# Attention of a two-layer decoder step: the low halves of the split keys are stored by GpSimd instead of SyncE

## The chip, the core and the metric

The kernel runs on one core of a Trainium2 chip. The metric is the device time of one execution in microseconds (us); for the kernel before it is 1973.53 us, the median of three runs from 1971.57 to 1974.1 us. An execution with the hardware profiler gives the views that are quoted below; its own time was 1971.77 us, its span from first to last instruction 1970.0 us.

## The reference

One inference step of a two-layer trunk on 1024 new prompt tokens and 8 sample tokens (one new token each for eight old sequences), width 1024. Layer 0 is a gated linear recurrence, layer 1 grouped-query attention over a window of 128 tokens, 16 query heads on 4 key heads of 64 channels, with a learned sink per head; a squared-ReLU MLP with 4096 hidden channels follows each. The part that the change touches is the norm of queries and keys and the product of the two:

```python
def qkv_heads(x, w_qkv, q_g, k_g):
    q, k, v = jnp.split(x @ w_qkv, [Q_DIM, Q_DIM + KV_DIM], axis=-1)
    q = rms_norm(q.reshape(n, t, N_KV, GROUP, HEAD_DIM), q_g)
    k = rms_norm(k.reshape(n, t, N_KV, HEAD_DIM), k_g)
    v = v.reshape(n, t, N_KV, HEAD_DIM)
...
    s = jnp.einsum('...qkgd,...skd->...kgqs', q, k).astype(jnp.float32) * (HEAD_DIM ** -0.5)
    s = s - alibi_slopes()[:, :, None, None] * dist.astype(jnp.float32)
    s = jnp.where(mask, s, NEG_INF)
```

Everything is float32.

## The kernel before

**Layout.** Activations lie with channels on the 128 partitions and the 1032 tokens (1024 and 8) along the free axis, eight tiles for the width. The tokens are worked on in three thirds of 344 columns (`cs(c)` is the slice of third c). Float32 products are made of float32r pieces: each operand is split into a high part (a cast, on ScalarE, called ACT in the profile) and a low part (the value less the high part, on VectorE, called DVE), and a product is three matmuls, high by high, high by low and low by high (`passes`, line 229).

**Weights.** They come from HBM in units of 128x1024, 512 KB, in one fixed order: for the attention k 0, q 0, k 1, v 0, v 1, q 1, q 2 and so on to q 7. `fetch` (line 166, the DMA is at L173) loads a unit into a tile `raw` from a ring of two buffers, issued by SyncE (SP); `split_unit` (line 175) makes the parts, in two halves each: a cast on ACT (L179) and a subtraction on DVE (L180). `ensure` and `unit` (lines 210 and 221) keep this some units ahead of the products. So the third unit in a row can be loaded only when the first has been split.

**Start of the attention.** `proj_many` (line 259, called at line 1140) projects, for each third in turn, the first pair of key heads (k 0) and then the first query tile (q 0): 24 matmuls each, recorded at L240. Then `proj_steps` (line 922, matmuls at L928) projects the second pair of key heads (k 1), third by third; `by_token` (line 357) computes factors for the values; `v_proj` (line 948, matmuls at L958) the values; and from line 1147 on the query tiles 1 to 7 are projected in between the blocks of the attention (`stage_a`, line 994, matmuls of queries by keys at L1003).

**What follows a projected third of keys.** `take_out` (line 843) takes it out of its bank by two instructions on ACT, a square (L845) and a copy (L846). `k_norm` (line 849) sums the squares of a head with a plain float32 matmul (L852), then DVE L853, ACT L306, L307, L308 and DVE L309, L311 make the factor. `k_evac` (line 901) multiplies (DVE L911), and `parts` (line 861) splits into `hi` (ACT L863) and the low part, which is left in `x` itself (DVE L864). Each part is then stored four times by DMAs from SBUF to SBUF (L915): the two heads of the pair (`own`, 64 partitions each) are each put into the lower and the upper half of a tile of their own, `kh` for the high and `kl` for the low parts. These are the tiles that L1003 reads. There are 2 pairs, 3 thirds and 8 stores of 86.0 KB for each: 48 stores. A projected third of queries goes through `q_evac` (line 870): a square (L875), a cast `hi` (L877), the low part `lo` (DVE L878), and four stores into the query tiles (L884, L885).

**What sets the order.** Each engine takes its instructions in program order, and the scheduler of the framework writes that order: it puts all instructions that are ready into a simulated order by priority, so an edit on one queue can move instructions on others. A DMA stands in the order of the engine that issues it, and waits there for its source, its target and its semaphore (8 of them in rotation for the DMAs of SP and ACT, 8 for those of GpSimd, called POOL). The small tiles of 128x344 (`S`: squares, `x`, `hi`, `lo`, factors) share 9 buffers; a buffer is free again when the stores that read it have landed.

Of the kernel before, what the change touches and what calls it, by code (L numbers as in the profile page):

```python
# [65 lines left out]
def trunk(ctx: ExitStack, tc: tile.TileContext, I, O):  # L66
    nc = tc.nc
    pe, act, dve, pool, sp = nc.tensor, nc.scalar, nc.vector, nc.gpsimd, nc.sync
# [36 lines left out]
    def A(s="a"):  # L105
        return A2(s)[:, 0:T]
# [4 lines left out]
    def S(s="s"):  # L111
        return small["pool"].tile([P, CH], F32, tag="S", name=nm(s))
# [27 lines left out]
    def cs(c):  # L140
        return slice(c * CH, (c + 1) * CH)
# [683 lines left out]
    def attention(hs):  # L825
# [23 lines left out]
        def k_norm(sx, e):  # L849
            s, x = sx  # L850
            st = B("N")[:, :CH]
            pe.matmul(st, lhsT=blk, rhs=s, start=True, stop=True)  # L852
            dve.scalar_tensor_tensor(s, e, fx["e4"], st, ALU.mult, ALU.add)  # L853
            return x, rstd_m2(s, eps=fx["e2"])

        kst = {}
# [4 lines left out]
        def parts(x):  # L861
            hi = S("hi")
            last["k act"] = act.copy(r_(hi), x).ins  # L863
            last["k dve"] = dve.tensor_tensor(r_(x), x, hi, ALU.subtract).ins  # L864
            return hi, x
# [35 lines left out]
        def k_evac(p, c, o, e):  # L901
            if c == 0:
                kst[p] = [(A("kh"), A("kl")) for _ in range(2)]
            x, r = k_norm(o, e)
            if c == 2:
                o = 2 * CH
                kout = S("kout")[:, :P + NS]
                dve.scalar_tensor_tensor(kout, x[:, SEQ - P - o:T - o], fx["kg"], r[:, SEQ - P - o:T - o], ALU.mult, ALU.mult)
                sp.dma_start(O["k"][p], kout[:, :P])
                pool.tensor_copy(ks[:, p, :], kout[:, P:P + NS])  # L910
            dve.scalar_tensor_tensor(x, x, qg[:, 0:1], r, ALU.mult, ALU.mult)  # L911
            for n, x in enumerate(parts(x)):
                for u, own in enumerate((lower, upper)):
                    for half in (lower, upper):
                        sp.dma_start(kst[p][u][n][half, cs(c)], x[own, :])  # L915
            if c == 2:
                done.add(("k", p))

# [219 lines left out]
        with tc.issue_after(last["c0"]):  # L1138
            wk, wq = unit("k", 0, 1), unit("q", 0, 1)
        proj_many([wk, wq], hs, lambda i, c, o: q_evac(0, c, o) if i else k_evac(0, c, take_out(o), fx["row"][:, cs(c)]))  # L1140
        run(proj_steps(unit("k", 1, 1), lambda c, o: k_evac(1, c, take_out(o), fx["row"][:, cs(c)]), iter(())))
        by_token()
        v_proj()
# [44 lines left out]
        for j in range(NJ):  # L1188
# [6 lines left out]
            n = max(0, int((j + 1 - j1) * r) - int((j - j1) * r)) if j < J0 or j >= J1 else 0  # L1195
# [375 lines left out]
```

## Time and profile before

| what | value |
|---|---|
| median of the runs | 1973.53 us (1971.57 to 1974.1, 3 runs) |
| profiled execution | 1971.77 us, span 1970.0 us |
| TensorE (PE) busy | 1958.6 us, 99% of the span |
| DVE, ACT, POOL busy | 1493.6, 1009.1, 363.9 us |
| the 48 stores of L915 | issued by SP from 988.2 to 1032.5 us, about 0.59 us each, landing 2.1 us after the issue (median) |
| PE from 985 to 1045 us | busy 57.66 of 60 us |

A row of a timeline gives the start in us from the begin of the span, the duration in us, the engine, the line of the kernel, the operation with its output and inputs (buffer numbers left out) and the count of merged instructions; in brackets stands how long the engine was idle just before, and what it waited for. "SPq" is SP issuing. A busy PE can still be a PE in which matmuls overlap: the start of one to the start of the next is what a matmul costs. A row of waits gives who waited, for whom, the total, the times and the longest. The landing of a DMA is counted from its issue.

### The profile page before, as it was taken

What the parts mean: (1) busy time and instruction counts of PE and PEld (TensorE: products, weight loads), DVE (VectorE), ACT (ScalarE), POOL (GpSimd) and SP (SyncE); (2) the same over time, 40 slices, a digit from 0 to 9 for tenths busy, and PEclk for the clock granted to TensorE, in tenths of its full rate; (3) what the DMA queues carried; (4) which work ended last, traced back from release to release, by engine and by line L of the source; (5) the groups of instructions that cost most, each with busy time, mean ns of one, the idle gap of its engine ahead of it and who ended that gap; (6) DMA issues with size and microseconds to landing.
All of it is one profiled execution on the core that took longest, in us unless ns stands there. A gap on an engine that the chain in (4) does not pass through costs nothing.

```text
span 1970.0 us, 34847 instructions
## 1 busy us (share of the span) xinstructions
PE 1958.6 (99%) x13004; PEld 1828.2 (93%) x13004; DVE 1493.6 (76%) x3006; ACT 1009.1 (51%) x1985; POOL 363.9 (18%) x618
## 2 busy tenths in 40 slices
PE   9999999999999999999999999999999999999999
PEld 9999999999999899999999998999999999999998
DVE  8896747987777888777744778579877779688784
ACT  6476636443434655554544667455443436455552
POOL 2330000000001233321003667100000003223321
PEclk9999999999999999999999999999999999999999
DMA  5111242244445798988353335612444447788886
GB/s 183 43 44 54 78 156 83 108 153 154 144 153 196 215 243 209 238 199 202 123 143 90 109 89 192 216 65 86 173 140 156 140 176 261 200 205 220 225 207 180
DMA packets 116537, 308.07 MB, mean 156 GB/s; under 512 B 17544, under 2 KB 47248, under 8 KB 116368
## 3 DMA queue, kind: packets, MB, share of 16 engines
q0 software_dynamic: 29568, 102.07, 21.6%
q1 hardware_dynamic: 56272, 131.34, 20.4%
q10 hardware_dynamic: 30528, 72.45, 10.3%
q8 instruction: 102, 1.67, 0.3%
q14 instruction: 67, 0.55, 0.1%
HBM read 177.95 MB, written 115.16 MB: 149 GB/s over the span
## 4 chain that ended last, share of the span: by engine, by line
PE 94%; DVE 2%; DMA 2%; ACT 1%; issue 1%; SPq 0%; POOL 0%; DVEq 0%; ACTq 0%
PE bD L605 36%; PE bZ L605 26%; PE bP L240 11%; PE bS L240 7%; PE bP L928 4%; PE bT L240 3%; PE bS L1003 2%; PE bO L1053 1%; PE bS L958 1%; PE bT L1030 1%; PE bP L1030 1%; DMA x<-xT 0%; PE bN L890 0%; DVE sq L291 0%; DVE hl L1256 0%
## 5 line engine op out<-in xcount | busy, mean ns | idle before, releaser
L605 PEld LDWEIGHTS bD<-op,op 128*128 128x128 f32 x3072 | 380.6, 188 | 8.1 <-DVE ho L753 0.3
L605 PE MATMUL bD<-op,op 128*128 128x260 f32 x3072 | 383.2, 283 | 0.0
L605 PEld LDWEIGHTS bD<-tl,op 128*128 128x128 f32 x2880 | 362.3, 188 | 11.8 <-DVE ho L753 0.6
L605 PE MATMUL bD<-tl,op 128*128 128x260 f32 x2880 | 366.5, 283 | 0.1
L618 POOL DMA_DIRECT2D tl<-hsum x210 | 123.6, 661 | 892.0 <-PE bD L605 409.8
L452 ACT CAST op<-ws 128x512 fp32r<-128x512 f32 (+2 forms) x288 | 158.7, 561 | 248.7 <-DVE ws L573 125.2
L605 PE MATMUL bZ<-op,op 128*128 128x512 f32 x1152 | 282.3, 395 | 0.8 <-DVE y L414 0.8
L605 PE MATMUL bZ<-tl,op 128*128 128x512 f32 x1080 | 272.2, 395 | 0.2 <-DVE tl L460 0.2
L605 PEld LDWEIGHTS bZ<-op,op 128*128 128x128 f32 x1152 | 210.6, 188 | 44.5 <-DVE y L414 1.1
L605 PEld LDWEIGHTS bZ<-tl,op 128*128 128x128 f32 x1080 | 194.6, 188 | 37.8 <-DVE tl L460 0.7
L460 DVE TENSOR_TENSOR tl<-tl 128x520 fp32r<-128x520 f32 (+1 forms) x210 | 136.5, 692 | 76.7 <-ACT tl L459 76.5
L452 ACT CAST op<-raw 128x512 fp32r<-128x512 f32 (+2 forms) x216 | 120.9, 561 | 133.8 <-PE bD L605 71.5
L453 DVE TENSOR_TENSOR op<-ws,op 128x512 fp32r<-128x512 f32 (+2 forms) x288 | 171.4, 610 | 7.6 <-ACT op L452 7.5
L453 DVE TENSOR_TENSOR op<-raw,op 128x512 fp32r<-128x512 f32 (+2 forms) x216 | 131.6, 611 | 9.6 <-ACT op L452 8.7
L753 DVE TENSOR_TENSOR ho<-bD,ho 128x520 f32<-128x520 f32 x140 | 97.5, 696 | 37.0 <-PE bD L605 36.1
L459 ACT CAST tl<-tl 128x520 fp32r<-128x520 f32 (+1 forms) x210 | 117.6, 626 | 2.2 <-DMA tl<-hsum 0.8
L180 DVE TENSOR_TENSOR wl<-raw,wh 128x512 fp32r<-128x512 f32 (+1 forms) x73 | 64.3, 895 | 35.9 <-ACT wh L179 19.2
L743 DVE TENSOR_TENSOR ho<-bZ,ho 128x512 f32<-128x512 f32 x72 | 49.6, 688 | 43.8 <-PE bZ L605 43.5
L727 ACT COPY he<-bZ 128x512 f32<-128x512 f32 x72 | 42.0, 583 | 75.4 <-PE bZ L605 69.4
L745 ACT COPY he<-bZ 128x512 f32<-128x512 f32 x68 | 39.9, 586 | 77.5 <-PE bZ L605 65.3
L753 DVE TENSOR_TENSOR he<-bD,he 128x520 f32<-128x520 f32 x71 | 49.4, 696 | 38.9 <-PE bD L605 38.7
L1016 ACT ACTIVATE se<-se,den 128x257 f32<-128x257 f32 (+1 forms) x128 | 62.9, 494 | 30.0 <-DVE den L1013 22.6
(365 smaller groups left out, 3950.7 us busy)
## 6 DMA issues: line engine op xcount, KB each, us to landing
raw<-w_up SPq DMA_DIRECT2D x64, 512.0 KB, 3.8
tl<-hsum POOLq DMA_DIRECT2D x120, 260.0 KB, 6.7
raw<-w_dn SPq DMA_DIRECT2D x64, 384.0 KB, 6.9
tl<-hsum POOLq DMA_DIRECT2D x90, 256.0 KB, 6.7
spill<-ho POOLq DMA_DIRECT2D x32, 516.0 KB, 6.7
spill<-he POOLq DMA_DIRECT2D x32, 516.0 KB, 6.5
hsum<-ts ACTq DMA_DIRECT2D x30, 520.0 KB, 4.0
hsum<-ho ACTq DMA_DIRECT2D x30, 516.0 KB, 3.6
```

What stands on the lines that cost most here:

```text
L180: eng.tensor_tensor(r_(lo[:, sl]), raw[:, sl], hi[:, sl], ALU.subtract)
L240: pe.matmul(o, lhsT=r_(wt[:, col(k):col(k) + P]), rhs=r_(xt[:, cs(c)]), start=(k == first and a == 0), stop=(k == final and a == 2))
L452: act.copy(r_(hi), x)
L453: dve.tensor_tensor(r_(lo), x, hi, ALU.subtract)
L459: act.copy(r_(hi), lo)
L460: eng.tensor_tensor(r_(lo), lo, hi, ALU.subtract)
L605: pe.matmul(d[:, 512 * b:512 * b + c], lhsT=r_(wt[:, j * P:j * P + P]), rhs=r_(xt[:, c * b:c * b + c]), start=first and j == 0 and a == 0, ...
L618: pool.dma_start(t[:, n:2 * n], src)
L743: dve.tensor_tensor(o0, d, o[:, HP], ALU.add)
L753: last["sum"] = dve.tensor_tensor(t, inner(d), t, ALU.add).ins
L928: pe.matmul(o, lhsT=r_(wt[:, k * P:k * P + P]), rhs=r_(xt[:, cs(c)]), start=(k == 0 and a == 0), stop=(k == M8 - 1 and a == 2))
L1016: act.activation(se[:, u, 256 - n:257], se[:, u, 256 - n:257], AF.Exp, scale=-1.0, bias=dn[:, u:u + 1], accum_out=dn[:, 2 + u:3 + u])
```

## The change

The four stores of a low part (`n` is 1 in the loop over `parts`) are issued by GpSimd, those of the high part by SP as before. 24 of the 48 stores move; what they copy is the same.

```diff
@@ -912,7 +912,7 @@
             for n, x in enumerate(parts(x)):
                 for u, own in enumerate((lower, upper)):
                     for half in (lower, upper):
-                        sp.dma_start(kst[p][u][n][half, cs(c)], x[own, :])
+                        (pool if n else sp).dma_start(kst[p][u][n][half, cs(c)], x[own, :])
             if c == 2:
                 done.add(("k", p))
```

The scheduler's order moves with it. On SP, at the first third of k 0 and q 0: `kh_10468` to `kl_10471` are the key tiles, `q_10519` and `q_10520` the query tiles, and `raw_10885` is the unit q 1 of the weights, which PE needs only for the second query tile.

```order
 L915 DMA kh_10470<-hi_10483 64x344 x2
-L915 DMA kl_10469<-x_10465 64x344 x2
-L915 DMA kl_10471<-x_10465 64x344 x2
+L173 DMA raw_10885<-w_qkv 128x1024
 L884 DMA q_10519<-hi_10523 64x344
 L885 DMA q_10519<-lo_10524 64x344
 L884 DMA q_10520<-hi_10523 64x344
 L885 DMA q_10520<-lo_10524 64x344
-L173 DMA raw_10885<-w_qkv 128x1024
```

The load of the unit q 1 now stands right behind the four stores of the high part; it stood behind four more of the low part and four of the query.

On ACT, in the second third: `wh_10895` is the high part of that unit q 1, `sq_10521`, `hi_10571` and `hi_10608` belong to the second third of q 0 and k 0, `sq_10641` and `x_10642` are the square and the copy of the last third of k 0.

```order
 L308 ACTIVATE q_10564<-r_10563 128x344
+L179 CAST wh_10895<-raw_10885 128x512 x2
 L875 ACTIVATE sq_10521<-bT_10582 128x344
 L863 CAST hi_10571<-x_10557 128x344
 L877 CAST hi_10608<-bT_10582 128x344
-L179 CAST wh_10895<-raw_10885 128x512 x2
 L845 ACTIVATE sq_10641<-bP_10616 128x344
 L846 COPY x_10642<-bP_10616 128x344
```

The two casts of the unit q 1, which stood right ahead of the square of the last third, stand three instructions earlier.

On PE, in the last third of q 0 (`bP_10671`), the matmul L852 of that square stands two matmuls earlier; the order of DVE is the same throughout. On POOL the stores fill a stretch that held only the copies of the last keys (L910):

```order
 L355 DMA st<-msrow 8x1
+L915 DMA kl_10469<-x_10465 64x344 x2
+L915 DMA kl_10471<-x_10465 64x344 x2
+L915 DMA kl_10469<-x_10557 64x344 x2
+L915 DMA kl_10471<-x_10557 64x344 x2
 L910 COPY st<-kout_10655 128x8
+L915 DMA kl_10469<-x_10642 64x344 x2
+L915 DMA kl_10471<-x_10642 64x344 x2
```

Further on in ACT's order, where the second third of k 1 is taken out, the row of the changed kernel with its waits reads as follows; DMASW are the semaphores of POOL's DMAs, and before the change this copy had no wait of its own.

```order
L845 ACTIVATE sq_10795<-bP_10770 128x344 [waits DMAHW3_49,DMAHW2_49,DMAHW4_49,DMAHW1_49,PE_49]
L846 COPY x_10796<-bP_10770 128x344 [waits DMASW3_49,DMASW4_49,DMASW2_49,DMASW1_49]
L306 ACTIVATE q_10803<-sq_10795,st 128x344 [waits DMAHW7_49,DMAHW5_49,DVE_49]
```

The copy L846 now waits for four stores of POOL, which hold the buffer that it writes.

## The prediction

> **What bounds the kernel now.** I read the busy times first, then the chain that ended last, then what PE waits for.
>
> ```profile
> span 1970.0 us, 34847 instructions
> PE 1958.6 (99%) x13004; PEld 1828.2 (93%) x13004; DVE 1493.6 (76%) x3006; ACT 1009.1 (51%) x1985; POOL 363.9 (18%) x618
> PE 94%; DVE 2%; DMA 2%; ACT 1%; issue 1%; SPq 0%; POOL 0%; DVEq 0%; ACTq 0%
> ```
>
> PE is busy for 1958.6 of 1970.0 us, and 94% of the chain is PE. Whatever does not shorten an idle stretch of PE is worth nothing, so the question is where those 11.4 us lie and whether the stores of L915 have a part in one. The first row of PE's waits over the whole run and the two windows around the stores answer it:
>
> ```profile
> PE bN L852 <- ACT sq L845: 2.2, 2, 2.1
> ```
>
> ```profile
> 985.00:1045.00 60.00, 57.66 (x407) 54.83 (x406) 24.07 (x50) 26.19 (x59) 0.62 (x3) 1.00 0.52 129
> 1045.00:1100.00 55.00, 55.00 (x400) 52.92 (x399) 32.99 (x137) 30.57 (x97) 26.95 (x56) 1.00 0.35 92
> ```
>
> The largest single wait of PE in the run, 2.1 us, is in the stage of the stores. The first row says that PE idles 60.00 − 57.66 = 2.34 us there; the second that it idles not at all in the next 55 us (first time column busy PE), at a granted clock of 1.00. So this stage can win about 2.3 us and no more, and what it wins is kept, since PE sets the pace behind it. PE's timeline shows the place:
>
> ```profile
> 990.44 0.32 PE L240 MATMUL bT<-hh,wh 128*128 128x344 f32 x1
> 991.15 0.85 PE L852 MATMUL bN<-sq,con 128*128 128x344 f32 x2
> ...
> 994.97 0.32 PE L240 MATMUL bP<-hh,wh 128*128 128x344 f32 x1
> ...
> 998.75 0.32 PE L240 MATMUL bP<-hh,wh 128*128 128x344 f32 x1
> ...
> 999.54 0.32 PE L240 MATMUL bP<-hh,wl 128*128 128x344 f32 x1
> 1001.93 0.85 PE L852 MATMUL bN<-sq,con 128*128 128x344 f32 x2 [2.08 <-ACT sq L845]
> ...
> 1005.46 0.32 PE L928 MATMUL bP<-hh,wh 128*128 128x344 f32 x1
> ```
>
> The second third of q 0, with the L852 of the keys within it, runs from 990.44 to 994.97, 4.53 us; the same work for the last third from 998.75 to 1005.46, 6.71 us. The difference, **2.18 us**, is what the stall costs. On ACT, at the same time:
>
> ```profile
> 995.18 0.46 ACT L875 ACTIVATE sq<-bT 128x344 f32<-128x344 f32 x1 [0.90 <-PE bT L240]
> 996.08 0.48 ACT L863 CAST hi<-x 128x344 fp32r<-128x344 f32 x1 [0.45 <-DVE x L911]
> 996.47 0.44 ACT L877 CAST hi<-bT 128x344 fp32r<-128x344 f32 x1
> 1000.39 1.14 ACT L179 CAST wh<-raw 128x512 fp32r<-128x512 f32 x2 [3.48 <-DMA raw<-w_qkv]
> 1001.43 0.45 ACT L845 ACTIVATE sq<-bP 128x344 f32<-128x344 f32 x1
> ```
>
> The square L845 that PE needs stands behind the two casts L179 of the weights q 1, and these wait 3.48 us for a load. The chain and SP's timeline tell why the load is late:
>
> ```profile
> 995.92 4.45 DMA raw<-w_qkv
> ```
>
> ```profile
> 988.25 2.46 SPq L915 DMA_DIRECT2D kh<-hi  x4
> 990.87 2.39 SPq L915 DMA_DIRECT2D kl<-x  x4
> ...
> 995.92 0.54 SPq L173 DMA_DIRECT2D raw<-w_qkv  x1
> 996.59 2.38 SPq L915 DMA_DIRECT2D kh<-hi  x4
> ```
>
> It is issued only after twelve stores, at 995.92, and lands 4.45 us later at 1000.37. So weights for the second query tile, which comes only after the values, hold a square that PE needs at once, because SP issues one DMA per 0.6 us.
>
> **The change part by part.** *The load.* With the new order on SP it follows the first four stores, where `kl` stood: 990.87 instead of 995.92, 5.05 us earlier. Its buffer must be free by then:
>
> ```profile
> 988.46 0.51 DVE L864 TENSOR_TENSOR x<-x,hi 128x344 fp32r<-128x344 f32 x1
> 988.89 0.51 DVE L878 TENSOR_TENSOR lo<-bS,hi 128x344 fp32r<-128x344 f32 x1
> 989.31 1.89 DVE L180 TENSOR_TENSOR wl<-raw,wh 128x512 fp32r<-128x512 f32 x3
> ```
>
> Of these three L180 the first (to 989.94) is the last reader of that buffer; even the third ends at 991.20, 0.3 us after the issue. Landing: the bounds over all loads of L173 are
>
> ```profile
> DMA to landing us min/median/max: 2.8/4.8/8.4
> ```
>
> I take 4.45 us, the same load's own row, so 995.32; the ends are 993.67 and 999.27.
>
> *ACT.* The casts stand three instructions earlier now. They start at 995.34 and end at 996.48 (1.14); L875, L863 and L877 behind them take at most 0.46 + 0.48 + 0.44 = 1.38, to 997.86, about 1 us later than today. The square L845 can start as soon as its bank is full: in the second third L852 starts 991.15 − 990.44 = 0.71 behind the first matmul of q 0, so 998.75 + 0.71 = 999.46, and L845 0.50 ahead of it (1001.93 − 1001.43), at 998.96. ACT is free 1.10 us before that: the load may land up to 996.42, 5.55 us after its issue, at no cost. The later `hi` of the second third costs nothing either: PE's matmuls of k 0 up to 998.75 cover it, and without that cover its 1 us would be added to the stall.
>
> *PE.* L852 starts at 999.46 instead of 1001.93, and the last third of q 0 ends 4.53 us after 998.75, at 1003.28 instead of 1005.46. **Sum: −2.18 us.** What comes next late is already there and stays: each third of k 1 waits for the norm of the one before, which contains no DMA:
>
> ```profile
> 1014.92 0.48 ACT L863 CAST hi<-x 128x344 fp32r<-128x344 f32 x1 [1.85 <-DVE x L911]
> 1015.31 0.45 ACT L845 ACTIVATE sq<-bP 128x344 f32<-128x344 f32 x1
> 1015.65 0.44 ACT L846 COPY x<-bP 128x344 f32<-128x344 f32 x1
> 1017.30 0.58 ACT L306 ACTIVATE q<-sq,st 128x344 f32<-128x344 f32 x1 [1.21 <-DVE sq L853]
> ```
>
> All four move 2.2 us ahead with PE.
>
> *POOL.* It gets 24 issues in a stretch in which it does almost nothing (0.62 busy of 60 us in the first window). No row of before shows a store of 86 KB from POOL; the nearest ones are its loads of 256 to 260 KB (first row its issues in ns, second its landings), its small copy of 4 KB, and the same store from SP:
>
> ```profile
> L618 POOL DMA_DIRECT2D tl<-hsum x210: 536/544/928, 623.4 to 1902.6; - x105
> ...
> DMA to landing us min/median/max: 2.9/6.7/9.6
> ```
>
> ```profile
> st<-msrow POOLq DMA_DIRECT2D x1, 4.0 KB, 2.9
> ```
>
> ```profile
> kl<-x SPq DMA_DIRECT2D x24, 86.0 KB, 2.1
> ```
>
> So an issue costs 0.54 us (up to 0.93), and a landing lies between 2.1 and 9.6 us; I take 2.9, the small copy's row, since 86 KB moved by SP in 2.1 is nearer to that than to the queue of large loads in a stage with busy DMA engines. By the Trainium skill's page "DMA: Bandwidth & Descriptors", section "Anatomy of one DMA — SWDGE (gpsimd) path", a DMA issued by GpSimd takes about 2.0 us and its bytes at 436 GB/s, an estimate of 2.2 us for 86 KB, by which the sum is the same. The tightest user is the copy L846 in the second third of k 1, which waits for four POOL stores; I take the latest that it can mean, those of the last third of k 0. There the low part in `x` is ready today at 1008.30:
>
> ```profile
> 1007.78 0.52 DVE L864 TENSOR_TENSOR x<-x,hi 128x344 fp32r<-128x344 f32 x1 [0.55 <-ACT hi L863]
> ```
>
> With L852 2.47 us earlier that is 1005.83; the last of four issues starts at 1007.5 and lands at 1010.4. L846 is due at 1015.65 − 2.18 = 1013.47, and may start as late as 1014.7 before it holds L306 (1017.30 − 2.18, less 0.44). So a landing of 7.2 us is still free; the value taken is 4.3 us away from it. The stores themselves are read by L1003 at 1058, so their own lateness costs nothing.
>
> *Sum.* 1971.77 − 2.18 = 1969.59 us for the profiled execution, which lies 1.76 us below the median of the runs. A fixed term comes off every run alike, so the median goes to 1973.53 − 2.18 = **1971.35 us**, 0.11% faster.
>
> **The rivals.** *A, the load lands late.* The POOL stores now run beside it, not behind it, and the DMA engines carry a mean share of 0.52 in this stage. Each us beyond 5.55 takes one of the gain, down to nothing at 7.7 us. At the bound of 8.4 it lands at 999.27, the casts end at 1000.43, the three behind them at 1001.81, L845 starts 0.38 later than today's 1001.43, and two matmuls of 0.16 that PE now has behind L852 come on top: 0.7 us slower, 1974.2. For it speaks the median of 4.8, against it that 4.45 was measured with twelve stores just ahead of the load in the same queue, where now only four are. Between no gain and all of it: 1972.4.
>
> *B, POOL's stores land late (the slower end).* If a landing takes 9.6 us and an issue 0.93, the last store of the four starts at 1008.6 and lands at 1018.2, L846 is 3.5 us beyond 1014.7, and the square behind that norm, on which PE already waits (1015.31 is such a square, right behind its L863), is later by as much: 3.5 − 2.18 = 1.3 us slower, 1974.8. It decides from a landing of about 8.3 us with these issues. Against it stand the page's row of the DMA engines in 40 slices of 49 us (tenths busy), and the slices in which L618 issues its loads:
>
> ```profile
> DMA  5111242244445798988353335612444447788886
> ```
>
> ```profile
> busy tenths in 40 slices 0000000000001222310000000000000002212210
> ```
>
> The large loads of POOL ran mostly in the slices with 7 to 9, the stores run in slice 21 with a 5. The Trainium skill's page "SBUF — State Buffer", section "Who interferes with whom", speaks against the change here: a DVE instruction in a two-port mode locks GpSimd out for its whole length, descriptors included. The row of 210 issues beside a DVE that is 76% busy shows 0.54 us in the median and 0.93 at most, so the trace bears out no lock beyond a few tenths of a us. By that rule B would come about with each issue held for a DVE instruction; the same 1974.8 is then its price.
>
> *C, nothing changes.* The order says the load moves; if its issue waited for the third L180 (991.20) that is 0.3 us, inside A's slack. A run without the gain would need ACT to wait for something else, such as a buffer of `hi`: 1973.5.
>
> *D, more than the stall.* All of PE's idle time in the stage is 2.34 us; 1971.2 at best from it. More than that would be noise between runs.
>
> **How the numbers follow.** Forecast 1971.4: 0.72. A: 0.12, C: 0.06, B: 0.07, D: 0.03. About 0.2%, 3.9 us, is what a measurement of this kernel can tell from no change; forecast, A, C and D lie within it. B at its price is 1.3 us, so only a POOL far slower than any row (a landing past 12 us) gets beyond. The runs of before spread over 2.5 us by themselves. Faster by over 0.2%: 0.07 (2.18 with 1.8 us of spread); slower by over 0.2%: 0.07; within: 0.86. The range: from the lowest run of before less the gain, 1971.57 − 2.18 = 1969.4, rounded out to 1969.2, up to A's bound of 1974.2, rounded out to 1974.4.
>
> **What would show it.** Right: the load of q 1 issued at about 990.9 and landed by 996.4; no wait of PE for L845 above 0.3 us; the first L928 at about 1003.3; POOL's 24 issues near 0.55 us with landings of 2 to 4 us; PE's idle time from 985 to 1045 about 0.2 us. Wrong: a wait of ACT L846, or of DVE, for `kl<-x`; a load of w_qkv that takes over 5.6 us; or a PE idle stretch somewhere behind 1045 that was not there.

## The result and the profile after

| | before | after |
|---|---|---|
| median of the runs | 1972.46 us (21 runs, 1970.31 to 1974.10) | 1969.62 us (21 runs, 1968.67 to 1970.26) |
| profiled execution | 1971.77 us, span 1970.0 | 1969.62 us, span 1967.8 |
| ratio | | 0.9986, 95% interval 0.9980 to 0.9992 |

The changed kernel is 0.14% faster: 2.8 us, with an interval of 1.6 to 3.9 us. By the bound of 0.2% that is no change, and by the interval it is still a real gain. The profiled executions differ by 2.15 us, and the spread of the runs falls from 3.8 to 1.6 us. One run among all that follow, of the kernel with the twenty stores, was in a slower state of the chip (3740.92 us at a granted clock of 0.93); the ratios leave it out, and without it the median of that kernel would be 1970.88 us in place of 1971.03.

The rows of the profile of after that answer to those of before: span and busy times, then the two windows around the stores (first time column busy PE), then PE's waits over the whole run.

```profile
span 1967.8 us, 34874 instructions
PE 1958.0 (100%) x13004; PEld 1826.8 (93%) x13004; DVE 1493.0 (76%) x3006; ACT 1009.0 (51%) x1985; POOL 375.2 (19%) x642
```

```profile
985.00:1045.00 60.00, 59.76 (x422) 57.00 (x421) 24.15 (x50) 26.13 (x59) 12.80 (x26) 1.00 0.47 129
1045.00:1100.00 55.00, 55.00 (x403) 52.66 (x403) 35.63 (x148) 32.08 (x102) 29.32 (x62) 1.00 0.38 105
```

```profile
PE bN L1232 <- POOL warm L1230: 1.1, 1, 1.1
PE bN L298 <- DVE sq L296: 1.1, 2, 0.8
PE bZ L605 <- DVE y L414: 0.8, 1, 0.8
PE bZ L605 <- ACT he L727: 0.7, 1, 0.7
```

PE's idle time in the stage of the stores falls from 2.34 to 0.24 us, and the stage behind it has none, as before. The wait of L852 for the square, first of the waits of before, is gone from the list; a row that before did not have is the fourth, 0.7 us of L605 for `he`, more than 900 us later. Nearly all of POOL's 12.80 us in the first window are the new issues.

Where the stall was, on SP, ACT and PE in this order:

```profile
987.78 2.47 SPq L915 DMA_DIRECT2D kh<-hi  x4
990.34 0.54 SPq L173 DMA_DIRECT2D raw<-w_qkv  x1
990.99 0.46 SPq L884 DMA_DIRECT2D q<-hi  x1
```

```profile
995.29 1.14 ACT L179 CAST wh<-raw 128x512 fp32r<-128x512 f32 x2 [1.49 <-DMA raw<-w_qkv]
...
997.06 0.45 ACT L877 CAST hi<-bT 128x344 fp32r<-128x344 f32 x1
998.47 0.46 ACT L845 ACTIVATE sq<-bP 128x344 f32<-128x344 f32 x1 [0.97 <-PE bP L240]
```

```profile
998.99 0.84 PE L852 MATMUL bN<-sq,con 128*128 128x344 f32 x2
...
1002.81 0.32 PE L928 MATMUL bP<-hh,wh 128*128 128x344 f32 x1
```

The load follows the first four stores, its data are there 4.95 us later, the casts run ahead of L875 and L877, and in front of the square ACT idles 0.97 us until PE has filled the bank. L852 carries no wait. The first stores stand 0.47 us earlier than in before (987.78 against 988.25), from stages that the change does not touch; counted from there, the first L928 comes 15.03 us later in place of 17.21, and that is 2.18 us.

### The profile page after: what moved, and what is told of

Its sections match the earlier page's. It is cut to its first block, busy times and chain, and to the rows that moved or that the text cites. A ratio compares the mean times of both kernels' runs of the same rounds, so it can differ in the third digit from the quotient of the medians.

```text
span 1967.8 us, 34874 instructions
## 1 busy us (share of the span) xinstructions
PE 1958.0 (100%) x13004; PEld 1826.8 (93%) x13004; DVE 1493.0 (76%) x3006; ACT 1009.0 (51%) x1985; POOL 375.2 (19%) x642
## 3 DMA queue, kind: packets, MB, share of 16 engines
q8 instruction: 102, 1.67, 0.4%
## 4 chain that ended last, share of the span: by engine, by line
PE 95%; issue 1%; DVE 1%; DMA 1%; ACT 1%; POOL 0%; SPq 0%; DVEq 0%; ACTq 0%; POOLq 0%
PE bD L605 35%; PE bZ L605 26%; PE bP L240 12%; PE bS L240 7%; PE bP L928 4%; PE bT L240 3%; PE bS L1003 2%; PE bO L1053 1%; PE bS L958 1%; PE bT L1030 1%; PE bP L1030 1%; PE bN L890 0%; DVE sq L291 0%; DMA o_y<-he 0%; DMA raw<-w_in 0%
## 5 line engine op out<-in xcount | busy, mean ns | idle before, releaser
L605 PEld LDWEIGHTS bD<-op,op 128*128 128x128 f32 x3072 | 380.6, 188 | 7.9
L605 PE MATMUL bD<-op,op 128*128 128x260 f32 x3072 | 383.1, 282 | 0.0
L605 PEld LDWEIGHTS bD<-tl,op 128*128 128x128 f32 x2880 | 362.2, 188 | 11.9 <-DVE ho L753 0.6
L605 PE MATMUL bD<-tl,op 128*128 128x260 f32 x2880 | 366.5, 282 | 0.1
L605 PE MATMUL bZ<-op,op 128*128 128x512 f32 x1152 | 282.3, 394 | 0.8 <-DVE y L414 0.8
L605 PE MATMUL bZ<-tl,op 128*128 128x512 f32 x1080 | 272.2, 395 | 0.9 <-ACT he L727 0.7
L605 PEld LDWEIGHTS bZ<-op,op 128*128 128x128 f32 x1152 | 210.4, 188 | 44.7 <-DVE y L414 1.1
L605 PEld LDWEIGHTS bZ<-tl,op 128*128 128x128 f32 x1080 | 194.3, 188 | 38.9 <-ACT he L727 0.9
L727 ACT COPY he<-bZ 128x512 f32<-128x512 f32 x72 | 41.9, 583 | 76.5 <-PE bZ L605 69.5
```

The costliest lines, as they stand in the source:

```text
L605: pe.matmul(d[:, 512 * b:512 * b + c], lhsT=r_(wt[:, j * P:j * P + P]), rhs=r_(xt[:, c * b:c * b + c]), start=first and j == 0 and a == 0, ...
```

## The experiments

**Theories.** The first: one wait is removed. In before, two casts that nobody needs yet stand on ACT ahead of a square that PE needs at once, and wait for a load that twelve stores on SP hold back. The rival: two queues carry the stores better, so that tiles come free sooner in every third. Four of the runs repeat before unchanged; the other kernels do the whole computation too, with other queues, another order or other sizes of the stores.

### The casts later, all stores on SyncE

```
-            w = [unit("v", 0, 1), unit("v", 1, 1)]
+            w = [unit("v", 0, 1), unit("v", 1, 0)]
...
-                    act.activation(v, ps[...], AF.Copy, scale=...)
+                    last["v act"] = act.activation(v, ps[...], AF.Copy, scale=...).ins
+                if b2 == 0:
+                    with tc.issue_after(last["v act"]):
+                        ensure(index["q", 1])
```

> The kernel of before (all stores on SyncE, the load of the weight unit q 1 at its old place on the queue) with one edit: the two casts of that unit stand on ScalarE behind the first block of the value projection, where nothing waits for them early, in place of ahead of the square L845 of the last third. The first theory (the kernel of before loses its time to casts that wait for a late load and hold up the square) expects the whole gain without any store on GpSimd: the wait of PE L852 for ACT sq L845, 2.2 us in the profile of before, falls under 0.3, the load still lands at about 1000.4, and the time is 2.2 to 2.9 us under before, a ratio of 0.9985 to 0.9989, as after's 0.9986. The rival (the time comes from the stores themselves: two queues send them sooner, so that tiles come free and operands stand ready sooner) expects no gain, a ratio of 0.9995 to 1.0005, with the casts out of the way but the time spent elsewhere in the same stage. Price of the edit by the first theory: under 0.3 us, if the two casts meet ScalarE's work in the value projection.

Measured: 1969.36 us, ratio 0.9986, interval 0.9977 to 0.9994. SP, then ACT (lines behind L968 stand three further down in this kernel):

```profile
995.45 0.54 SPq L173 DMA_DIRECT2D raw<-w_qkv  x1
```

```profile
998.48 0.46 ACT L845 ACTIVATE sq<-bP 128x344 f32<-128x344 f32 x1 [2.03 <-PE bP L240]
...
1034.77 1.14 ACT L179 CAST wh<-raw 128x512 fp32r<-128x512 f32 x2
```

The load is as late as in before and all 48 stores are on SP, yet the square starts when its bank is full, and the whole gain is there. It needs no store on GpSimd; the rival's price for this kernel, no gain, falls.

### Four stores moved, or the other twenty

```
-  (pool if n else sp).dma_start(...)
+  (pool if n and (p, c) == (0, 0) else sp).dma_start(...)   first kernel: four
+  (pool if n and (p, c) != (0, 0) else sp).dma_start(...)   second kernel: twenty
```

> The kernel of before with only the four low-part stores of the first third of k 0 on GpSimd; the other twenty stay on SyncE. The load of the weight unit q 1 stands on SyncE ahead of the query stores, as in after, and the order on ScalarE and TensorE is after's. The first theory (one wait of the square, behind one load) expects the whole gain from these four: the load issued at about 990.3, no wait of PE L852 over 0.3 us, a time within 0.4 us of after's 1969.6, a ratio of 0.9984 to 0.9990. The rival (two queues carry the stores better, in each third) expects a sixth of the gain, 0.4 to 0.5 us, a ratio of about 0.9998.

> The other side of the kernel with four stores moved: the twenty low-part stores of the other five thirds are on GpSimd, the four of the first third of k 0 stay on SyncE, ahead of the load. The first theory expects none of the gain: the load issued at about 995.4 as in before, landing 3.9 to 4.5 us later at 999.3 to 999.9, PE L852 waiting 1.6 to 2.2 us for the square, and a ratio of 0.9993 to 1.0002. The rival (two queues) expects five sixths of the gain, a ratio of about 0.9988, and no wait of L852.

Measured: four stores, 1969.22 us, ratio 0.9986, interval 0.9977 to 0.9995; the other twenty, 1971.03 us, ratio 0.9995, interval 0.9986 to 1.0004. The casts in the kernel with four, then in the kernel with twenty, and PE's first wait in the latter:

```profile
995.87 1.14 ACT L179 CAST wh<-raw 128x512 fp32r<-128x512 f32 x2 [1.78 <-DMA raw<-w_qkv]
...
998.76 0.46 ACT L845 ACTIVATE sq<-bP 128x344 f32<-128x344 f32 x1 [0.68 <-PE bP L240]
```

```profile
1000.20 1.14 ACT L179 CAST wh<-raw 128x512 fp32r<-128x512 f32 x2 [3.38 <-DMA raw<-w_qkv]
1001.24 0.45 ACT L845 ACTIVATE sq<-bP 128x344 f32<-128x344 f32 x1
```

```profile
PE bN L852 <- ACT sq L845: 2.0, 1, 2.0
```

The four stores ahead of the load bring all that after has; twenty of the 24 leave the wait at 2.0 us. The median with the twenty is 0.6 us under before's 1971.67 in that series, an amount that the interval does not tell from nothing. The rival's shares of a sixth and five sixths are the wrong way round.

### How late the load may be

```
-            w = [unit("v", 0, 1), unit("v", 1, 1)]
+            with tc.issue_after(last["q st", 0, 0]): w = [unit("v", 0, 1)]
+            w.append(unit("v", 1, 1))
```

> The kernel of after with the stores on both queues, but the load of the weight unit q 1 is issued behind the four query stores of the first third, where it stood ahead of them; the casts go back to their place right ahead of the square L845. The first theory expects a part of the loss back, by the size of the delay: in after the query stores behind the load are issued to 993.5, so the load is issued at about 993 in place of 990.34, lands 4.5 to 4.9 us later at 997.4 to 997.9, both casts are done 1.1 us later at 998.5 to 999.0, the square follows at about 999.0 to 999.5 in place of 998.47, and PE L852 waits 0.5 to 1.0 us for it; the time is 0.4 to 1.0 us over after, a ratio against before of 0.9989 to 0.9992. The rival (stores on two queues) expects after's time, 0.9986, since every store is on the queue where after has it. A difference this small stands or falls with the wait in the profile more than with the time.

In the second kernel the queues are exchanged:

```
-  (pool if n else sp).dma_start(...)
+  (sp if n else pool).dma_start(...)
```

> The kernel of after with the queues exchanged: the high parts' stores by GpSimd, the low parts' by SyncE. The number of stores on each queue is after's. The low parts are ready later than the high ones, so on SyncE the query stores pass ahead of the load of the weight unit q 1, which is then issued at about 993.9 in place of 990.34, lands 4.5 to 4.9 us later at 998.4 to 998.8, and the casts, which stand right ahead of the square L845 again, end 1.1 us later at 999.5 to 999.9. The first theory expects PE L852 to wait 1.0 to 1.5 us and the time to be 0.9 to 1.5 us over after, a ratio against before of 0.9991 to 0.9994: about half of the gain is given back although just as many stores have left SyncE. The rival (fewer stores on a queue) expects after's time, 0.9986. A third reading, that a queue waits for whichever part is late whatever is behind it, would show as a wait of PE for the low parts, not for the square.

Measured: load later, 1969.29 us, ratio 0.9989, interval 0.9980 to 0.9998; queues exchanged, 1969.78 us, ratio 0.9988, interval 0.9979 to 0.9996. Both expectations of a partial loss missed. The ratio of the first kernel holds one run of 1974.77 us; its other ten lie between 1968.85 and 1969.98. The load and the casts of the first kernel, and of the second:

```profile
993.08 1.02 SPq L173 DMA_DIRECT2D raw<-w_qkv  x2
```

```profile
996.97 1.14 ACT L179 CAST wh<-raw 128x512 fp32r<-128x512 f32 x2 [0.56 <-DMA raw<-w_qkv]
998.44 0.46 ACT L845 ACTIVATE sq<-bP 128x344 f32<-128x344 f32 x1 [0.33 <-PE bP L240]
```

```profile
993.57 1.01 SPq L173 DMA_DIRECT2D raw<-w_qkv  x2
```

```profile
997.48 1.14 ACT L179 CAST wh<-raw 128x512 fp32r<-128x512 f32 x2 [1.16 <-DMA raw<-w_qkv]
998.53 0.45 ACT L845 ACTIVATE sq<-bP 128x344 f32<-128x344 f32 x1
```

The load was issued as late as expected (993.08 and 993.57), but its data were there after 3.9 us, not 4.5 to 4.9. So the casts ended before the square was due in the first kernel, with 0.33 us to spare, and just as it was due in the second: the square follows them without an idle gap there, and PE idles 0.31 us in the stage, against 0.24 in after. The missed expectations are about the size of the landing; by these two rows the threshold that they look for is at data ready by about 997.4, where the casts stand right ahead of the square. The kernel with the queues exchanged lies 0.4 to 0.5 us above the two others of its series (1969.36 with the casts later, 1969.29 with the load later); its stage accounts for less than 0.1 us of that, and the rest was not found.

### GpSimd's queue: more stores, smaller stores

All eight stores of a third on GpSimd (`pool.dma_start` for both parts):

> The kernel of after with the high parts' stores on GpSimd too: eight a third on GpSimd, none on SyncE. The load of the weight unit q 1 is then at most 2.5 us earlier (issued at about 988 to 990.3, as far as its tile is free), and the square is already unhindered in after. The first theory expects after's time, within 0.5 us of 1969.6, and the wait of L852 gone. GpSimd's time for eight issues is 8 x 0.52 = 4.2 us a third, against a third of 4.4 us, so its queue keeps up, and the kernel with four pieces showed that 96 issues of 0.52 us hinder nobody. A rival that counts a queue's load expects a loss: the low parts are issued behind the high ones, and the tiles hi and x of a third come free up to 2 us later, which would show as waits of ACT L863 or L846 for a store, and 0.5 to 2 us.

Each low-part store in four pieces of 86 columns:

```
-  (pool if n else sp).dma_start(kst[p][u][n][half, cs(c)], x[own, :])
+  for y in range(0, CH, CH // 4 if n else CH):
+      (pool if n else sp).dma_start(kst[p][u][n][half, cs(c)][:, y:y + (CH // 4 if n else CH)], x[own, y:y + (CH // 4 if n else CH)])
```

> The kernel of after with each low-part store cut into four stores of 86 columns, so that GpSimd issues 16 in place of 4 for each third (96 in place of 24, the same bytes). Both theories keep the load's gain; this one prices GpSimd's queue. In after an issue holds GpSimd 0.52 us and four of them 2.06 us; sixteen take 8.2 to 8.5 us, and the low part of the first third, ready at 988.8, is all issued at about 997.2, that of the second (x ready at about 998) at 1006.5, that of the third at 1015. The tile x of the second third of k 0 is wanted again by the copy L846 of the first third of k 1 only when its store has landed 2.7 us later. Expected from the rows: the queue falls behind by about 1 to 2 us a third, the first copies of k 1 wait for x, and 1 to 3 us are lost, a ratio against before of 0.999 to 1.000. If an issue of a quarter as many bytes takes a quarter of the time (0.13 us), nothing is lost and the ratio stays 0.9986: the price of an issue is then in bytes, not in instructions.

Measured: all on GpSimd, 1970.00 us, ratio 0.9989, interval 0.9980 to 0.9998, which is after's time within 0.4 us as the first theory had it, with 0.2 us of PE L852 waiting for the square and none for a store; four pieces, 1969.96 us, ratio 0.9990, interval 0.9981 to 0.9998. The stores by GpSimd in after (ns, least, median, most; first and last start), and in the kernel with four pieces; behind it POOL's timeline there:

```profile
L915 POOL DMA_DIRECT2D kl<-x x24: 517/522/568, 988.8 to 1027.3; - x24
...
DMA to landing us min/median/max: 2.3/2.7/5.0
```

```profile
L915 POOL DMA_DIRECT2D kl<-x x96: 517/522/568, 989.2 to 1040.2; - x96
```

```profile
997.15 10.28 POOL L915 DMA_DIRECT2D kl<-x  x20 [1.37 <-DMA kl<-x]
...
1007.71 24.67 POOL L915 DMA_DIRECT2D kl<-x  x48
```

An issue costs 522 ns whether it moves 86 or 21.5 KB, so between these two sizes the price is one of instructions, as the first half of the expectation had it. The second half missed: with 96 issues the queue is busy without a gap from 1007.71 to 1032.38, and still PE's waits name no store of it. The low parts are read by L1003, which starts at 1055.4 in after, and the copies L846 of k 1 found their tiles free. In this stage GpSimd has room for four times the issues. That they are free is not shown: the loss against after is about 0.3 us, less than two series of runs can tell apart, but against the kernel with four stores, from the same series, it is 0.74 us (1969.28 to 1970.84 against 1968.71 to 1969.93). PE idles 0.29 us in the stage there and 0.26 with the four stores, so this loss lies elsewhere; where was not found.

### Both edits together

The kernel of after with the diff of the first experiment:

> The kernel of after with the edit of the first experiment as well (the two casts of the weight unit q 1 stand behind the first block of the value projection). The first theory expects nothing more, a time within 0.4 us of after's 1969.6, a ratio of 0.998 to 0.9992 against before: both edits remove the same wait, and it can be removed once. If the two gains were separate (the stores' queues, and the casts' place), they would add, 2 us under after, a ratio of about 0.9975.

Measured: 1969.86 us, ratio 0.9988, interval 0.9979 to 0.9996. Nothing adds up: the two edits remove the same wait.

### Four more profiles of before

> The kernel of before once more, unchanged, for a second profile. The question is whether the landing of the load of the weight unit q 1 differs from run to run and passes straight into the end. In the first profile it took 4.45 us from issue at 995.92 and PE waited 2.2 us. The first theory expects the wait of PE L852 to follow the landing microsecond for microsecond: with a landing of 4.9 us, which is what the same load took in after, the wait is about 2.65 us and the profiled time about 0.5 us longer; it explains that the medians differ by 2.8 us where the two profiled executions differ by 2.15. If the landing is again within 0.1 us of 4.45, this doesn't explain the 0.7 us, and something outside the wait must.

> The kernel of before a third time, unchanged. The second profile had a wait of 2.0 us of PE L852 and 1.2 us of PE L605 for ACT he L727 near the end, which waits for the landing of a store of o_y; the first had 2.2 and none; after has none and 0.7. Expected: the wait of L852 is the landing time of the load less 2.2 to 2.3 us (4.45 gave 2.2, 4.26 gave 2.0), the wait for he L727 is between 0 and 1.2 us, and the profiled time follows the sum of the two: 1969.6 us, plus the wait of L852, plus 0 to 1.2 us, less what after itself waits, 0.7. A time of over 1973 with both waits within these bounds would show a third place where runs of before differ.

> The kernel of before a fourth time, unchanged. Its timed runs fall into a larger group at 1970.5 to 1972 and a smaller one at 1973 to 1974; the three profiles so far (1971.77, 1972.62, 1971.1) have waits of 2.2, 2.0 and 1.8 us of PE L852 and 0, 1.2 and 0 us of PE L605 for ACT he L727. Expected: 1969.4 us, within 0.3, plus these two waits. Where the time is over 1973, the sum of the two should be over 3.3 us; if it isn't, a third place differs from run to run.

> The kernel of before a fifth time, unchanged. Expected as for the fourth: 1969.4 us, within 0.3, plus the wait of PE L852 and the wait of PE L605 for ACT he L727.

Measured, in the order of the wait (the second column runs from the issue of the load on SP to the start of the casts on ACT):

| profile of before | issue to casts | PE L852 waits | PE L605 for `he` L727 | profiled time |
|---|---|---|---|---|
| first | 4.47 us | 2.08 us | 0 | 1971.77 us |
| second | 4.27 | 1.88 | 1.18 | 1972.62 |
| third | 4.21 | 1.79 | 0 | 1971.10 |
| fourth | 4.07 | 1.67 | 0 | 1970.92 |
| fifth | 4.01 | 1.59 | 0 | 1971.15 |

The casts and PE's wait in the fifth:

```profile
999.59 1.14 ACT L179 CAST wh<-raw 128x512 fp32r<-128x512 f32 x2 [3.00 <-DMA raw<-w_qkv]
```

```profile
1001.13 0.85 PE L852 MATMUL bN<-sq,con 128*128 128x344 f32 x2 [1.59 <-ACT sq L845]
```

The wait is the landing less 2.4 us in each, so the landing passes straight into PE's wait. The time is that wait plus the one for `he`, on a base of 1969.3 to 1969.7, as the last two expectations had it. The second wait hangs on another transfer, a store of `o_y` by GpSimd. Its landing in the first profile of before, in the second, and in after:

```profile
o_y<-he POOLq DMA_DIRECT2D x1, 516.0 KB, 4.1
```

```profile
o_y<-he POOLq DMA_DIRECT2D x1, 516.0 KB, 5.1
```

```profile
o_y<-he POOLq DMA_DIRECT2D x1, 516.0 KB, 5.0
```

At 4.1 us PE waits nothing, at 5.1 it waits 1.2, at 5.0 in after 0.7. It differs from run to run with the same kernel, and the kernel with the casts later, whose stores of L915 are all on SP, has 0.5 us of it too; so after's new row in the list of waits needs no store on GpSimd. That a kernel without the stall meets it more often is not excluded: seven of the eight profiles without the stall show it, two of the six with it.

The explanation by a longer landing failed: all four repeats had a shorter one than the first profile. The five profiles give a wait of 1.6 to 2.1 us, and the medians differ by 2.8 (2.65 and 2.45 in the series with the first experiment and with the four stores). Of the 96 timed runs of before in the four series 26 lie above 1972.9 us, none of the five profiles does, and of the 43 runs of after, of the casts later and of the four stores none lies above 1970.3. What happens in those 26 runs stays open: the two waits together would have to come to 3.3 us or more, and the most that a trace shows is 3.06, in the second profile.

Two things on record narrow it. The long runs go with the wait: of the 106 runs of before and of the kernel with the twenty stores, which both have it, 27 lie above 1972.9 us; of the 98 runs of the kernels without it one does, the 1974.77 us of the kernel with the load later, and at 1971.1 us, a bound lower by the wait, two do. And they go with a lower mean granted clock of TensorE: it is noted for 75 runs of before, 18 of them above 1972.9 us, and 17 of these 18 show 0.998 or 0.999, against 8 of the other 57. A clock lower by 0.001 over 1970 us would be 2.0 us, an estimate, and about the distance. This is a lead and not a cause. Of the runs without the wait 19 show 0.999 and are not long, and in the profile of the casts later, whose mean is also 0.999, the clock is 1.00 through the stage of the stores and 0.71 only from 1964 to 1968, where PE has no matmul left.

## Why the prediction was right

The forecast was 1971.4, from a median of 1973.53, with a range of 1969.2 to 1974.4; 1969.62 came out, only 0.4 us above the lower end. By its steps:

- **The place.** One wait of PE in the stage, all of it for the square behind two casts: shown, by the casts later on one queue, and by four stores against twenty.
- **The load.** Issued at 990.34 for 990.87; less the 0.47 us that the stage began earlier, 0.06 off. The landing was mis-sized: 4.45 taken, 4.95 measured to the start of the casts (5.27 in the kernel with four stores). The margin took it: data allowed up to 5.55 us behind the issue, and 0.97 us of ACT's idle time was left, since the three instructions behind the casts ended at 997.51, 2.22 us after the casts began, not 2.52.
- **PE.** L852 at 998.99 and the first L928 at 1002.81 against 999.46 and 1003.28: both the 0.47 us earlier, and otherwise exact. The stall's −2.18 us is what was measured from the first stores on. The profiled execution came out at 1969.62 for 1969.59, with two errors that nearly cancel: 0.5 us were gained ahead of the change and 0.7 lost to `he` behind it. The first is from run to run (the first stores of the five profiles of before start between 987.78 and 988.25); that they meet so closely is luck.
- **POOL.** 24 issues of 522 ns for 0.54, landings of 2.7 us in the median for 2.9 in the sum and 2.2 in the prediction's other estimate; at 2.3 to 5.0 some were above the 2 to 4 that it named. No copy L846 waited. One sign of being wrong, a wait of DVE for `kl<-x`, does stand in the profile of after. Before has such a row as well, and the same instruction one third earlier in after, which names ACT, waits as long, 1.70 us; so it is the usual wait within the norm, put down to a store that landed during it. The row of before, then two of after:

```profile
1013.10 0.58 DVE L309 SCALAR_TENSOR_TENSOR q<-sq,st,q 128x344 f32<-128x344 f32 x1 [1.70 <-DMA kl<-x]
```

```profile
1010.46 0.58 DVE L309 SCALAR_TENSOR_TENSOR q<-sq,st,q 128x344 f32<-128x344 f32 x1 [1.70 <-ACT q L308]
...
1016.33 0.58 DVE L309 SCALAR_TENSOR_TENSOR q<-sq,st,q 128x344 f32<-128x344 f32 x1 [1.70 <-DMA kl<-x]
```

- **Rival A** (the load late): the landing was in fact the longer one, and cost nothing; the twenty stores show what a load behind `kl` costs, 2.0 us. **Rival B** (POOL's stores late): a landing of at most 5.0 us against its 8.3, and even 96 issues did not bring it about. The lock of the Trainium skill's page "SBUF — State Buffer", section "Who interferes with whom", would show as long issues: at most 568 ns here, beside a DVE that has 24.15 busy us in the window. Which of those DVE instructions work in a two-port mode no run here shows, so the lock itself is not tested. **Rival C** fell with the first trace.
- **Rival D** (more than the stall) had a chance of 0.03 and is the nearest to the medians: 2.8 us is more than the 2.34 of all idle time. The step that was off is "a fixed term comes off every run alike": the stall of one profile, 2.18 us, was carried over to the median, and it differs from run to run. It was not too small as profiles show it, since the four later ones have shorter waits (1.59 to 1.88 us). What the sum lacks are the runs of before above 1972.9 us, 8 of the 21 in this series: the median of the other 13 is 1971.51 us, 1.9 us above after's. Why they are long no profile caught.

The medians of the first three runs of before, 1973.53, and of 21, 1972.46, differ by 1.07 us; the forecast as a time was 1.8 us too high, 1.07 of it from this base and the rest, 0.7, from the gain.

## What to carry to other kernels

When an engine that paces nothing holds up the one that does, look at what stands ahead of the late instruction in its own order, and then at what stands ahead of that one's data in a DMA queue: here one load behind four stores too many cost 2 us, and the other twenty stores cost nothing that could be measured. Moving the cast or moving the stores is worth the same, once; before moving 24 stores, ask which of them stand ahead of something urgent. A stall that ends with a transfer's landing is a spread, not a number: take it from several profiles before it is carried over to a median.

## What the hardware showed unasked

A small store behind a large load on the same queue lands later. The query stores behind the load of 512 KB, in before (where those of the first third stand ahead of it) and in after, over the stage:

```profile
q<-hi SPq DMA_DIRECT2D x6, 86.0 KB, 2.1
q<-lo SPq DMA_DIRECT2D x6, 86.0 KB, 2.1
```

```profile
raw<-w_qkv SPq DMA_DIRECT2D x4, 512.0 KB, 4.8
q<-hi SPq DMA_DIRECT2D x6, 86.0 KB, 3.8
q<-lo SPq DMA_DIRECT2D x6, 86.0 KB, 3.7
```

Before has it as well, for the key stores right behind the load (issued from 996.59 on; first row) against those of the first third (second row):

```profile
kh<-hi SPq DMA_DIRECT2D x3, 86.0 KB, 4.1
```

```profile
kh<-hi SPq DMA_DIRECT2D x3, 86.0 KB, 2.0
```

Once, in after, this reached an engine, without consequence for PE: DVE waited 0.41 us for a tile that such a store still read.

```profile
1005.76 0.52 DVE L878 TENSOR_TENSOR lo<-bP,hi 128x344 fp32r<-128x344 f32 x1 [0.41 <-DMA q<-lo]
```

The load itself was slower where it was issued early, right behind the first four key stores with query stores following (4.95 and 5.27 us to the casts), than where it stood behind the query stores (3.9 in the two kernels with the load later, 4.0 to 4.5 in the profiles of before). In the kernel with four pieces, where the next load stands between it and the query stores, it took 4.45. Whether the transfers behind it or those ahead of it decide this was not tried by itself.
